# Three seven-product groups in each feed-forward step, and weight sums made by adding DMAs

## The chip, the cores and the metric

The kernel runs on one NeuronCore of a Trainium2 chip. The metric is the device time of one execution in microseconds. The kernel before takes 1654.93 us, the median of three runs (1654.54 to 1655.04).

## The reference

A two-layer encoder trunk on 256 tokens of 1024 channels, in float32. Each layer is a half-weighted feed-forward step, a mixer (an RG-LRU, a retention and a short convolution, gated and summed) and a second half-weighted feed-forward step; there are four feed-forward steps in all.

```python
def swiglu(u, w_in, w_out):
    gate, up = jnp.split(u @ w_in, 2, axis=-1)
    return (jax.nn.silu(gate) * up) @ w_out

for l in range(DEPTH):
    h = swiglu(rmsnorm(x, ffn1_pre_g[l]), ffn1_w_in[l], ffn1_w_out[l])
    x = x + 0.5 * rmsnorm(h, ffn1_post_g[l])
    h = hybrid_mixer(rmsnorm(x, mix_pre_g[l]), positions, ...)
    x = x + rmsnorm(h, mix_post_g[l])
    h = swiglu(rmsnorm(x, ffn2_pre_g[l]), ffn2_w_in[l], ffn2_w_out[l])
    x = x + 0.5 * rmsnorm(h, ffn2_post_g[l])
```

`w_in` is 1024 x 5632 (gate and up, 2816 each), `w_out` 2816 x 1024.

## The kernel before

**Precision.** Every float32 operand of a product is split into two parts: `hi`, the value cast to the matmul's format, and `lo`, the rest. A product is three matmuls (`mm3`, L457): hi x hi, hi x lo, lo x hi. Activations are split when they are transposed (`split`, L442), weights when they have been loaded.

**The weight stream.** All weights pass as 128x1024 units in one fixed order through the class `Stream`. `prep` (L153) loads a unit (two units per 1 MB DMA on SP's queue, tile `raw`), casts it on ACT to `whi` (L171) and subtracts on DVE to `wlo` (L172). There are eight buffers of each; `done` gives units back when the work that reads them has been written, and `fill` preps the next ones, at most eight ahead of the oldest that is still held.

**A feed-forward step** (`ffn`, L481) has eleven slices of 256 hidden channels. For a slice and one of the two token blocks of 128, `fin` is the input product (24 matmuls of 128x512 into one PSUM bank `psin`), `gate_up` the Silu on ACT and the product with up on DVE, `ftr` the transpose and split to `hl`, and `fout` the output product (12 matmuls into `psacc`, which collects over all slices). A slice's input costs 48 matmuls, its output 24. An input slice is four units, an output slice two.

**Seven products for eight.** For two slices c and d = c + 1, `block` computes the input product of the two token blocks, seen as a 2x2 times 2x2 block product, with seven products of 12 matmuls (P1 to P7, `product`, L519) in place of eight (2 x 48 = 96 matmuls). It needs four sums of the activations (`make_sums`, L350: two tiles `s`, each split again) and four sums of the weights. The weight blocks b[0] to b[3] are loaded as halves of 128x1024 into tiles `gw` (and one `w4`), and `part` (L178) forms the sums on DVE (L190 to L194) when P6 and P4 are prepped: four sums for each of two halves in each group. There are two groups in a step, (2, 3, 4, 5) and (6, 7, 8, 9) in `BLOCKS`, each with two slices a and b in the plain form between the products; slices 0, 1 and 10 are plain too. The results of the products are put together by `second`, `sixth`, `fifth` and `fourth` on DVE.

**What sets the order.** `ffn_plan` gives the order of the units, the code of `ffn` and `block` the order of the work; a scheduler then places the instructions in one queue per engine, and each engine runs its queue in that order. `turn` (an argument of `ffn`) transposes and splits the second token block of the step's input, and `first_sums` does the activation sums in the first step. POOL has only the powers of the RMS norms (L311, L389) and, in the first step, the constants of the LRU (`channel_consts`, L708); it issues no DMA.

## Time and profile before

| What | Value |
|---|---|
| Median of three runs | 1654.93 us |
| The profiled execution | 1654.75 us, its span 1653.0 us |
| PE busy | 1642.4 us (99% of the span), 7559 instructions |
| DVE busy | 1244.4 us (75%) |
| ACT busy | 920.7 us (56%) |
| POOL busy | 49.0 us (3%) |
| Moved by DMA | 309.85 MB, mean 187 GB/s |

PE is TensorE's matmul row, DVE the vector engine, ACT the scalar engine, POOL GpSimd, SP the engine that issues the weight loads. Busy matmuls overlap, so a busy share of 99% says that PE hardly waits, not that it is at its peak. The transposes of `turn` and their like (L370) stand in the chain of waits at 202.84, 657.22, 838.23, 1020.49 and 1475.10 us: the feed-forward steps take about 0 to 205 us, 650 to 838, 838 to 1020 and 1470 to 1653 of the span, and a mixer follows the first step of each layer.

### The profile page before, as it was taken

What the parts mean: (1) busy time and instruction counts of PE and PEld (TensorE: products, weight loads), DVE (VectorE), ACT (ScalarE), POOL (GpSimd) and SP (SyncE); (2) the same over time, 40 slices, a digit from 0 to 9 for tenths busy, and PEclk for the clock granted to TensorE, in tenths of its full rate; (3) what the DMA queues carried; (4) which work ended last, traced back from release to release, by engine and by line L of the source; (5) the groups of instructions that cost most, each with busy time, mean ns of one, the idle gap of its engine ahead of it and who ended that gap; (6) DMA issues with size and microseconds to landing.
All of it is one profiled execution on the core that took longest, in us unless ns stands there. A gap on an engine that the chain in (4) does not pass through costs nothing.

```text
span 1653.0 us, 19707 instructions
## 1 busy us (share of the span) xinstructions
PE 1642.4 (99%) x7559; PEld 1353.5 (82%) x7559; DVE 1244.4 (75%) x1596; ACT 920.7 (56%) x1249; POOL 49.0 (3%) x71
## 2 busy tenths in 40 slices
PE   9999999999999999999999999999999999999998
PEld 7888888888888888888888888888888888888886
DVE  7978779976666657878789777798566556688785
ACT  6556577654545445555556555766445545465553
POOL 0130000000000000000000000000000000000000
PEclk9999999999999999999999999999999999999999
DMA  9643554555454465464465444545554454645631
GB/s 332 245 180 147 207 177 174 208 183 204 159 197 153 179 241 204 169 239 176 170 240 191 153 153 179 203 153 208 200 196 161 170 186 155 256 169 185 215 109 69
DMA packets 50206, 309.85 MB, mean 187 GB/s; under 512 B 5696, under 2 KB 6080, under 8 KB 18112
## 3 DMA queue, kind: packets, MB, share of 16 engines
q1 hardware_dynamic: 47808, 301.18, 49.9%
q10 hardware_dynamic: 2304, 7.41, 1.2%
q8 instruction: 59, 0.97, 0.2%
q14 instruction: 35, 0.29, 0.1%
HBM read 307.52 MB, written 1.05 MB: 187 GB/s over the span
## 4 chain that ended last, share of the span: by engine, by line
PE 97%; DVE 2%; ACT 1%; issue 0%; DVEq 0%; POOLq 0%; ACTq 0%
PE psin L460 21%; PE psin L459 21%; PE psin L458 21%; PE psacc L458 9%; PE psacc L460 9%; PE psacc L459 9%; PE pstr L506 1%; PE pstr L773 1%; PE pstr L370 1%; DVE wlo L172 1%; PE pstr L941 0%; PE pstr L1020 0%; ACT whi L171 0%; PE psacc L290 0%; PE pstr L460 0%; PE pstr L458 0%
## 5 line engine op out<-in xcount | busy, mean ns | idle before, releaser
L172 DVE TENSOR_TENSOR wlo<-raw,whi 128x1024 fp32r<-128x1024 f32 x500 | 599.0, 1220 | 246.0 <-ACT whi L171 237.4
L171 ACT CAST whi<-raw 128x1024 fp32r<-128x1024 f32 x500 | 517.1, 1052 | 265.2 <-PE psacc L460 140.5
L458 PE MATMUL psin<-whi,uh 128*128 128x512 f32 x1424 | 561.0, 394 | 0.0
L459 PE MATMUL psin<-wlo,uh 128*128 128x512 f32 x1424 | 557.4, 391 | 0.5 <-DVE small L310 0.5
L460 PE MATMUL psin<-whi,ul 128*128 128x512 f32 x1424 | 556.9, 391 | 0.0
L460 PEld LDWEIGHTS psin<-whi,ul 128*128 128x128 f32 x1424 | 267.5, 188 | 55.6 <-DVE ul L445 0.5
L459 PEld LDWEIGHTS psin<-wlo,uh 128*128 128x128 f32 x1424 | 267.8, 188 | 54.1 <-DVE wlo L172 1.3
L458 PEld LDWEIGHTS psin<-whi,uh 128*128 128x128 f32 x1424 | 267.6, 188 | 53.2
L458 PE MATMUL psacc<-whi,hl 128*128 128x512 f32 x352 | 141.0, 401 | 0.9 <-ACT hl L444 0.5
L172 DVE TENSOR_TENSOR wlo<-gw,whi 128x1024 fp32r<-128x1024 f32 x96 | 116.1, 1220 | 30.3 <-ACT whi L171 30.3
L460 PE MATMUL psacc<-whi,hl 128*128 128x512 f32 x352 | 138.2, 393 | 0.0
L459 PE MATMUL psacc<-wlo,hl 128*128 128x512 f32 x352 | 137.5, 391 | 0.0
L171 ACT CAST whi<-gw 128x1024 fp32r<-128x1024 f32 x96 | 101.0, 1052 | 45.3 <-PE psin L460 24.7
L460 PE MATMUL psacc<-whi,spl 128*128 128x512 f32 x256 | 100.1, 391 | 0.0
L458 PE MATMUL psacc<-whi,spl 128*128 128x512 f32 x256 | 100.0, 390 | 0.0
L459 PE MATMUL psacc<-wlo,spl 128*128 128x512 f32 x256 | 99.8, 390 | 0.0
L458 PEld LDWEIGHTS psacc<-whi,hl 128*128 128x128 f32 x352 | 66.2, 188 | 15.3 <-ACT hl L444 3.4
L460 PEld LDWEIGHTS psacc<-whi,hl 128*128 128x128 f32 x352 | 66.1, 188 | 15.1 <-DVE hl L445 1.3
L459 PEld LDWEIGHTS psacc<-wlo,hl 128*128 128x128 f32 x352 | 66.3, 188 | 12.6
L311 POOL TENSOR_TENSOR small<-small,mhalf 128x1 f32<-128x1 f32 x38 | 29.5, 776 | 1521.9 <-DVE small L310 1521.0
L444 ACT CAST hl<-pstr 128x256 fp32r<-128x256 f32 x88 | 31.7, 370 | 55.2 <-PE pstr L506 55.2
L761 ACT COPY tok<-psin 128x512 f32<-128x512 f32 x40 | 23.4, 586 | 62.8 <-PE psin L460 62.8
(207 smaller groups left out, 1726.2 us busy)
## 6 DMA issues: line engine op xcount, KB each, us to landing
raw<-in_w_dram SPq DMA_DIRECT2D x250, 1024.0 KB, 4.8
gw<-in_w_dram SPq DMA_DIRECT2D x48, 512.0 KB, 6.9
w<-in_w_dram SPq DMA_DIRECT2D x16, 512.0 KB, 6.8
gain<-in_gains_dram ACTq DMA_DIRECT2D x10, 512.0 KB, 5.2
raw<-in_w_dram SPq DMA_DIRECT2D x8, 256.0 KB, 6.6
w<-in_gw_dram ACTq DMA_DIRECT2D x4, 512.0 KB, 3.4
x<-in_x_dram SPq DMA_DIRECT2D x2, 512.0 KB, 4.2
out_dram<-x SPq DMA_DIRECT2D x4, 256.0 KB, 2.1
```

Of the source, the lines that this page charges most:

```text
L171: (act or nc.scalar).copy(hi[:, c], raw[:, c])
L172: self.lows[i] = (dve or nc.vector).tensor_sub(lo[:, c], raw[:, c], hi[:, c].bitcast(F32))
L311: pool_e.tensor_tensor(r, r, mhalf, op=ALU.pow)
L370: pe.transpose(pt[:, i * P:(i + 1) * P], t[:, c * P:(c + 1) * P], ident)
L444: act.copy(h, src)
L458: pe.matmul(ps, lhsT=xh, rhs=wh, start=first, stop=False)
L459: pe.matmul(ps, lhsT=xh, rhs=wl, start=False, stop=False)
L460: pe.matmul(ps, lhsT=xl, rhs=wh, start=False, stop=last)
L506: pe.transpose(pt[:, i * P:(i + 1) * P], t[:, 256 + i * P:256 + (i + 1) * P], ident)
L761: act.copy(t, ps)
L773: pe.transpose(pt[:, i * SEQ + tb * P:i * SEQ + (tb + 1) * P], toks[tb][:, c * P:(c + 1) * P], ident)
```

## The change

There are three groups in each step, for the slice pairs (2, 3), (5, 6) and (8, 9), each with one plain slice a before it (1, 4, 7). The group with a = 1 comes first in the step and takes slice 0 into its order: P1 and P2 stand between the two token blocks of slice 0, and P3, P7 and P6 follow around slice 1. Another set of seven products is used. Per half it holds two tiles, x (from the block b11) and y (from b22), and z for b21, which is loaded whole into a `raw` tile. Weights of P1 are x, of P3 y, of P2 z. After P3's split a DMA that POOL issues adds b12 from memory into y; that is P7's operand. P6's is y + x, the one sum still made on DVE. After P6's split two more DMAs add b21 into y (for P4) and b12 into x (for P5). That is six adding DMAs of 512 KB in a group, 72 in all. The activation sums change their signs, and P1 to P7 are put together by other operations (`third`, `sixth`, `fifth`, `fourth`). In `channel_consts` the constants move from POOL to DVE, all but one power. `turn` is called within P2.

```diff
-PRODUCTS = (("P1", 2), ("P3", 0), ("P2", 3), ("P6", 2), ("P7", 0), ("P5", 1), ("P4", 3))
-SLOT = dict(PRODUCTS)
-BLOCKS = ((2, 3, 4, 5), (6, 7, 8, 9))
+PRODUCTS = ("P1", "P2", "P3", "P4", "P5", "P6", "P7")
+BLOCKS = ((1, 2, 3), (4, 5, 6), (7, 8, 9))
 def ffn_plan(blocks):
-    r, s = [], 0
-    while s <= NS:
-        block = [b for b in blocks if b[0] == s]
-        if block:
-            a, b, c, d = block[0]
-            r += [("in", a), ("P1", c), ("out", a - 1), ("P3", c), ("P2", c), ("in", b), ("P6", c), ("out", a),
-                  ("P7", c), ("out", b), ("P5", c), ("P4", c), ("out", c)]
-            s += 4
-            continue
-        if s < NS:
-            r.append(("in", s))
-        if s >= 1:
-            r.append(("out", s - 1))
-        s += 1
-    return r
+    r = [("in", 0)]
+    for a, c, d in blocks:
+        if a == 1:
+            r += [("P1", c), ("P2", c), ("in", a), ("P3", c), ("P7", c), ("P6", c), ("out", 0), ("out", a)]
+        else:
+            r += [("P3", c), ("P1", c), ("in", a), ("P7", c), ("P6", c), ("out", a - 1), ("P2", c), ("out", a)]
+        r += [("P4", c), ("P5", c), ("out", c)]
+    return r + [("in", NS - 1), ("out", NS - 2), ("out", NS - 1)]
...
             return piece
         piece(0)
-    def part(self, name, slot, half):
-        dve = self.nc.vector
-        if (name, half) == ("P1", 0):
-            self.group = [[None] * 4, [None] * 4]
-        b = self.group[half]
-        if name in ("P1", "P3"):
-            for k, q in enumerate((2, 0) if name == "P1" else (3, 1)):
-                b[q] = self.spare(name == "P3" and k == 1)
-                self.nc.sync.dma_start(b[q], self.w[self.pair, :, k * UW:(k + 1) * UW])
-            self.pair += 1
+        if kind is not None:
+            self.later(*kind)
+    def part(self, name, half):
+        if name in ("P1", "P3") and half == 0 and not self.open:
+            self.open = True
+            self.b11, self.b22, self.b21, self.b12 = [self.w[self.pair + k] for k in range(4)]
+            self.pair += 4
+            self.x, self.y = [None] * 2, [None] * 2
+        k = slice(half * UW, (half + 1) * UW)
+        if name == "P1":
+            self.x[half] = self.spare()
+            self.nc.sync.dma_start(self.x[half], self.b11[:, k])
+        elif name == "P3":
+            self.y[half] = self.spare()
+            self.nc.sync.dma_start(self.y[half], self.b22[:, k])
+        elif name == "P2":
+            if half == 0:
+                self.z = self.pool.tile([P, 2 * UW], F32, tag="raw", name=f"raw21_{self.pair}", bufs=RBUFS)
+                self.nc.sync.dma_start(self.z, self.b21)
+            return self.z[:, k]
         elif name == "P6":
-            dve.tensor_sub(b[0], b[0], b[1])
-            dve.tensor_sub(b[1], b[1], b[2])
-            dve.tensor_add(b[2], b[0], b[2])
-        elif name == "P4":
-            dve.tensor_sub(b[3], b[3], b[2])
-        return b[slot]
+            self.nc.vector.tensor_add(self.y[half], self.y[half], self.x[half])
+        return (self.x if name in ("P1", "P5") else self.y)[half]
+    def later(self, name, half):
+        def add(t, b):
+            self.nc.gpsimd.dma_start(t[half], b[:, half * UW:(half + 1) * UW], accum_op=ALU.add)
+        if name == "P3":
+            add(self.y, self.b12)
+        elif name == "P6":
+            add(self.y, self.b21)
+            add(self.x, self.b12)
+            self.open = False
...
         dve.tensor_sub(t[:, 0:2].rearrange("p c q t -> p q c t"), f, a)
-        dve.tensor_sub(t[:, 2], a[:, :, 1], t[:, 0])
-        dve.tensor_add(t[:, 1], t[:, 1], t[:, 0])
-        dve.tensor_add(t[:, 3], t[:, 2], f[:, :, 0])
+        dve.tensor_add(t[:, 2], t[:, 0], a[:, :, 1])
+        dve.tensor_sub(t[:, 1], t[:, 0], t[:, 1])
+        dve.tensor_sub(t[:, 3], t[:, 2], f[:, :, 0])
         h, lo = [tp.tile([P, 4, 2, P], F32R, tag="w4", name=nm("s"), bufs=8) for _ in range(2)]
         split(h, lo, t)
...
-        def block(a, b, c, d):
-            (u, v), (z, w) = halves(w4()), halves(w4())
+        def block(a, c, d):
+            (u, v), (z, w) = halves(w4()), [None] * 2
             def second(ps):
-                dve.tensor_add(z, u, ps)
-                gate_up(c, 0, [z])
+                t = v if a == 1 else u
+                dve.tensor_add(t, u, ps)
+                gate_up(c, 0, [t])
+            def third(ps):
+                nonlocal z, w
+                z, w = halves(w4())
+                act.copy(z, ps)
+            def fourth(ps):
+                dve.tensor_sub(z, ps, w)
+                gate_up(c, 1, [z])
+            def fifth(ps):
+                dve.tensor_sub(v, v, ps)
+                dve.tensor_sub(w, w, ps)
+                gate_up(d, 0, [v])
+                gate_up(d, 1, [w])
             def sixth(ps):
-                dve.tensor_add(u, u, ps)
-                dve.tensor_add(v, v, u)
-            def fifth(ps):
-                dve.tensor_add(v, v, ps)
-                dve.tensor_add(u, w, ps)
-                gate_up(d, 0, [v])
-                gate_up(d, 1, [u])
-            def fourth(ps):
-                dve.tensor_add(w, w, ps)
-                gate_up(c, 1, [w])
-            fin(a, 0)
-            fin(a, 1)
-            st.done(ui[a])
-            product(c, "P1", lambda ps: act.copy(u, ps))
-            fout(a - 1, 0)
-            ftr(a, 0)
-            fout(a - 1, 1)
-            ftr(a, 1)
-            st.done(uo[a - 1])
-            product(c, "P3", lambda ps: act.copy(v, ps))
-            product(c, "P2", second)
-            fin(b, 0)
-            fin(b, 1)
-            st.done(ui[b])
-            product(c, "P6", sixth)
-            fout(a, 0)
-            ftr(b, 0)
-            fout(a, 1)
-            ftr(b, 1)
-            st.done(uo[a])
-            product(c, "P7", lambda ps: dve.tensor_add(w, u, ps))
-            ftr(c, 0)
-            fout(b, 0)
-            fout(b, 1)
-            st.done(uo[b])
+                dve.tensor_sub(v, ps, u)
+                dve.tensor_sub(w, v, w)
+                dve.tensor_sub(v, v, z)
+            if a == 1:
+                product(c, "P1", lambda ps: act.copy(u, ps))
+                product(c, "P2", second, turn)
+                ftr(0, 0)
+                if start:
+                    first_sums()
+                else:
+                    fin(0, 1)
+                    st.done(ui[0])
+                fin(a, 0)
+                ftr(0, 1)
+                product(c, "P3", third)
+                ftr(a, 0)
+                fin(a, 1)
+                st.done(ui[a])
+                product(c, "P7", lambda ps: act.copy(w, ps))
+                product(c, "P6", sixth)
+                fout(0, 0)
+                ftr(c, 0)
+                fout(0, 1)
+                ftr(a, 1)
+                st.done(uo[0])
+                fout(a, 0)
+                fout(a, 1)
+                st.done(uo[a])
+            else:
+                product(c, "P3", third)
+                product(c, "P1", lambda ps: act.copy(u, ps))
+                fin(a, 0)
+                fin(a, 1)
+                st.done(ui[a])
+                product(c, "P7", lambda ps: act.copy(w, ps))
+                product(c, "P6", sixth)
+                fout(a - 1, 0)
+                ftr(a, 0)
+                fout(a - 1, 1)
+                ftr(a, 1)
+                st.done(uo[a - 1])
+                product(c, "P2", second)
+                fout(a, 0)
+                ftr(c, 0)
+                fout(a, 1)
+                st.done(uo[a])
+            product(c, "P4", fourth)
             product(c, "P5", fifth)
-            product(c, "P4", fourth)
             fout(c, 0)
+            ftr(c, 1)
             ftr(d, 0)
             ftr(d, 1)
-            ftr(c, 1)
             fout(c, 1)
             st.done(uo[c])
```

The order of the instructions, as the program has it. Names are tiles with their buffer numbers, DMASW is a semaphore of a DMA that POOL issued, DMAHW one of SP's or ACT's.

DVE in the first step, around the activation sums (`w_29`, `w_39`; `wlo` is a weight split). Before:

```order
L438 TENSOR_TENSOR w_28_313<-uh_115,ul_116 128x1024 [waits DVE_49]
L498 TENSOR_TENSOR tok_358<-psin_333,tok_358 128x256 [waits Activation_49]
L354 TENSOR_TENSOR w_29_315<-w_27_311,w_28_313 128x2x2x128 [waits DVE_49]
L445 TENSOR_TENSOR hl_364<-pstr_361,hl_364 128x256 [waits Activation_49]
L355 TENSOR_TENSOR w_29_315<-w_28_313,w_29_315 128x256 [waits DVE_49]
L356 TENSOR_TENSOR w_29_315<-w_29_315 128x256
L357 TENSOR_TENSOR w_29_315<-w_29_315,w_27_311 128x256 [waits DVE_49]
```

With the change (`gw_328` and `gw_335` are the halves of y):

```order
L447 TENSOR_TENSOR w_38_375<-uh_115,ul_116 128x1024
L454 TENSOR_TENSOR hl_370<-pstr_367,hl_370 128x256 [waits PE_49]
L165 TENSOR_TENSOR wlo_360<-gw_328,whi_359 128x1024 [waits DMASW0_49,Activation_49]
L363 TENSOR_TENSOR w_39_377<-w_37_373,w_38_375 128x2x2x128 [waits DVE_49]
L165 TENSOR_TENSOR wlo_364<-gw_335,whi_363 128x1024 [waits DMASW1_49,Activation_49]
L364 TENSOR_TENSOR w_39_377<-w_39_377,w_38_375 128x256 [waits DVE_49]
L365 TENSOR_TENSOR w_39_377<-w_39_377 128x256
L366 TENSOR_TENSOR w_39_377<-w_39_377,w_37_373 128x256 [waits DVE_49]
```

Both splits of P7, which wait for adding DMAs, now stand ahead of the three last operations of the activation sum.

DVE in the third feed-forward step (layer 1, the first step), where the results of products are put together and `hl`, the transposed hidden slices, are split. Before, in the first group:

```order
L545 TENSOR_TENSOR w_666_7213<-w_666_7213 128x512 [waits DVE_49]
L445 TENSOR_TENSOR hl_7532<-pstr_7529,hl_7532 128x256 [waits Activation_49]
L172 TENSOR_TENSOR wlo_7555<-gw_7271,whi_7554 128x1024 [waits Activation_49]
L445 TENSOR_TENSOR hl_7550<-pstr_7547,hl_7550 128x256 [waits Activation_49]
L172 TENSOR_TENSOR wlo_7560<-gw_7279,whi_7559 128x1024 [waits Activation_49]
L577 TENSOR_TENSOR w_667_7214<-w_666_7213,psin_7563 128x512 [waits PE_49]
```

With the change (`gw_7166`, `gw_7173` are y, for P4; `gw_6936`, `gw_6942` are x, for P5; `hl_7384` is slice 1 of the second token block):

```order
L165 TENSOR_TENSOR wlo_7320<-gw_7166,whi_7319 128x1024 [waits DMASW7_49,PE_49,Activation_49]
L165 TENSOR_TENSOR wlo_7324<-gw_7173,whi_7323 128x1024 [waits DMASW1_49,PE_49,Activation_49]
L571 TENSOR_TENSOR w_642_7046<-psin_7327,w_642_7046 128x512 [waits PE_49]
L165 TENSOR_TENSOR wlo_7344<-gw_6936,whi_7343 128x1024 [waits DMASW6_49,Activation_49]
L572 TENSOR_TENSOR w_667_7235<-w_642_7046,w_667_7235 128x512 [waits DVE_49]
L165 TENSOR_TENSOR wlo_7348<-gw_6942,whi_7347 128x1024 [waits DMASW0_49,Activation_49]
L573 TENSOR_TENSOR w_642_7046<-w_642_7046,w_667_7235 128x512 [waits DVE_49]
L454 TENSOR_TENSOR hl_7366<-pstr_7363,hl_7366 128x256 [waits Activation_49]
L454 TENSOR_TENSOR hl_7384<-pstr_7381,hl_7384 128x256 [waits Activation_49]
```

The weight splits near the `hl` rows waited for ACT alone; four that wait for adding DMAs now stand ahead of both.

POOL at the same place, before:

```order
L311 TENSOR_TENSOR small_6798<-small_6798,mhalf 128x1 [waits DVE_49]
L311 TENSOR_TENSOR small_6812<-small_6812,mhalf 128x1 [waits DVE_49,Pool_49]
L311 TENSOR_TENSOR small_6938<-small_6938,mhalf 128x1 [waits DVE_49]
L311 TENSOR_TENSOR small_6952<-small_6952,mhalf 128x1 [waits DVE_49,Pool_49]
L311 TENSOR_TENSOR small_8331<-small_8331,mhalf 128x1 [waits DVE_49,Pool_49]
```

With the change:

```order
L320 TENSOR_TENSOR small_6993<-small_6993,mhalf 128x1 [waits DVE_49]
L320 TENSOR_TENSOR small_7007<-small_7007,mhalf 128x1 [waits DVE_49,Pool_49]
L199 DMA gw_7166<-in_w_dram 128x1024 [waits DMASW4_49,DMAHW3_49,DVE_49,Activation_49]
L199 DMA gw_7173<-in_w_dram 128x1024 [waits DMASW5_49,DMASW2_49,DMAHW2_49,DVE_49,Activation_49]
L199 DMA gw_6936<-in_w_dram 128x1024 [waits DMAHW1_49,DMASW6_49,DVE_49]
L199 DMA gw_7166<-in_w_dram 128x1024 [waits DMASW7_49,DVE_49]
L199 DMA gw_6942<-in_w_dram 128x1024 [waits DMASW0_49,DVE_49]
L199 DMA gw_7173<-in_w_dram 128x1024 [waits DMASW1_49,DVE_49]
```

Between the powers of the norms POOL's queue now has the adds of the group, each behind a wait for DVE.

## Rows read from the trace of the kernel before

**Rows 1.** The page: span, engines' busy time, the weight queue, the chain by engine.

```profile
span 1653.0 us, 19707 instructions
...
PE 1642.4 (99%) x7559; PEld 1353.5 (82%) x7559; DVE 1244.4 (75%) x1596; ACT 920.7 (56%) x1249; POOL 49.0 (3%) x71
...
q1 hardware_dynamic: 47808, 301.18, 49.9%
...
PE 97%; DVE 2%; ACT 1%; issue 0%; DVEq 0%; POOLq 0%; ACTq 0%
```

**Rows 2.** Who waited for whom, PE alone: us in total, times, longest us.

```profile
PE psacc L290 <- DVE ones L287: 1.4, 1, 1.4
PE psin L127 <- DVE ul L127: 0.5, 1, 0.5
PE psacc L458 <- ACT hl L444: 0.5, 1, 0.5
PE psin L127 <- ACT uh L127: 0.5, 1, 0.5
PE psin L459 <- DVE small L310: 0.5, 2, 0.2
PE psin L127 <- DVE wlo L127: 0.2, 1, 0.2
```

**Rows 3.** Timeline of PE in the first step: start us, us, instruction.

```profile
23.49 0.49 PE L458 MATMUL psin<-whi,uh 128*128 128x512 f32 x1
23.82 0.39 PE L459 MATMUL psin<-wlo,uh 128*128 128x512 f32 x1
...
28.84 0.39 PE L460 MATMUL psin<-whi,ul 128*128 128x512 f32 x1
```

**Rows 4.** Timelines of ACT, then DVE, in the first step.

```profile
20.34 2.00 ACT L171 CAST whi<-raw 128x1024 fp32r<-128x1024 f32 x2
...
23.69 0.41 ACT L497 ACTIVATE tok<-psin 128x256 f32<-128x256 f32 x1
...
24.81 3.48 DVE L172 TENSOR_TENSOR wlo<-raw,whi 128x1024 fp32r<-128x1024 f32 x3
...
33.09 0.68 DVE L354 TENSOR_TENSOR w<-w,w 128x512 f32<-128x512 f32 x1
33.69 0.42 DVE L445 TENSOR_TENSOR hl<-pstr,hl 128x256 fp32r<-128x256 f32 x1
34.02 0.42 DVE L355 TENSOR_TENSOR w<-w,w 128x256 f32<-128x256 f32 x1
```

**Rows 5.** Weight loads: one tile's, then issues in windows 700:760 and 20:50, the page.

```profile
DMA to landing us min/median/max: 3.4/6.9/10.1
...
gw<-in_w_dram SPq DMA_DIRECT2D x6, 512.0 KB, 6.1
...
gw<-in_w_dram SPq DMA_DIRECT2D x4, 512.0 KB, 8.3
...
raw<-in_w_dram SPq DMA_DIRECT2D x250, 1024.0 KB, 4.8
```

**Rows 6.** Windows of the first step: busy by engine, granted clock, DMA share, GB/s.

```profile
25.00:30.00 5.00, 5.00 (x25) 4.10 (x24) 5.00 (x5) 3.95 (x6) 0.00 (x0) 1.00 0.96 354
30.00:35.00 5.00, 5.00 (x24) 4.06 (x23) 5.00 (x9) 3.52 (x5) 0.00 (x0) 1.00 0.99 359
```

**Rows 7.** Windows at the end, then the timeline of PE's opening.

```profile
1646.00:1647.00 1.00, 0.68 (x3) 0.20 (x2) 0.66 (x1) 0.59 (x3) 0.00 (x0) 1.00 0.00 0
...
1648.00:1649.00 1.00, 0.00 (x0) 0.00 (x0) 0.87 (x2) 0.00 (x0) 0.34 (x1) 0.88 0.00 0
1649.00:1650.00 1.00, 0.00 (x0) 0.00 (x0) 0.79 (x2) 0.00 (x0) 0.00 (x0) 0.50 0.03 10
...
1.44 6.25 PE L290 MATMUL psacc<-ones 128*128 128x512 f32 x15 [1.44 <-DVE ones L287]
7.53 1.04 PE L127 MATMUL pstr<-ident,w 128*128 128x128 f32 x8
```

93 lines of the change are left out of this document (35 added, 58 removed).

## The prediction

> **What bounds the kernel now.** Start with the page's first table [rows 1]: TensorE (PE) is busy 1642.4 us of a span of 1653.0, and the chain that ended last is 97% PE. DVE is at 75%, ACT at 56%, POOL at 3%. The view of who waited for whom, for PE alone [rows 2], lists six waits, the longest 1.4 us, at the start. So PE's instruction stream is the time: a matmul less is time less, and a wait of PE is time more. DVE and ACT work ahead of it; each weight unit is split there (cast to `whi`, subtract to `wlo`) up to eight units before PE reads it.
>
> The mean of one 128x512 matmul in the list of lines (391 ns) is no price, since matmuls overlap. In the timeline of PE the starts go from 23.82 to 28.84 with 22 steps between them [rows 3]: 5.02 / 22 = 0.228 us each. That is the price used here. In the same way the timelines of ACT and DVE give what one more instruction costs in a queue [rows 4]: a cast of a unit 0.95 us (two in 2.00), a 128x1024 subtract or add 1.14 (three in 3.48), a 128x512 operation 0.60, a 128x256 one 0.33. A transpose on PE costs 0.13 (eight in 1.04 [rows 7]).
>
> **What the change removes.** A seven-product group needs 84 matmuls where two slices need 96. There are two groups per feed-forward step before, three after, four steps: 4 x 12 = 48 matmuls less, 48 x 0.228 = 10.9 us. It is all on the path.
>
> **What costs nothing by itself.** DVE loses 40 weight sums (64 to 24) at 1.14 us, 45.6 us, and gets 24 unit splits more, 27.4 us; ACT gets 24 casts, 22.8 us. Neither engine is full, and the prefetch of eight units hides it; where it doesn't, it is in the deadlines below. The LRU constants come back to DVE as some 25 short operations in the first step; 1.0 us of them stands in a deadline below. `turn` keeps its place in time: 39 matmuls after the step's first one (24 + 15 before, 24 + 12 + 3 after). Loaded data grows by some 24 MB to about 334 MB, over queues that are used 50% [rows 1].
>
> **What it adds: 72 adding DMAs on POOL's queue, and waits for them.** No row of the trace shows such a DMA. Call L the time from the moment its last reader on DVE is done to its landing. The nearest rows are the plain 512 KB loads of the same tiles [rows 5]: 3.4 us at the fastest, 10.1 at the slowest; median 6.1 in a stretch inside a feed-forward step, 8.3 at the start, where the DMA engines are 0.96 to 0.99 busy [rows 6]. I take the medians of the place, 6.1 and 8.3, and keep 3.4 and 10.1 as the ends.
>
> In groups two and three P3 and P7 start 72 matmuls apart (16.4 us), and from P6's end to P4 there are 60 (13.7 us); no cost up to L = 10. The first group of each step is different: P3, P7 and P6 follow each other closely, and each is the last sum plus one more matrix.
>
> *Steps two to four* (time from the first matmul of slice 0). Slice 0 of the second token block ends after 72 matmuls and some ten transposes, 17.8. DVE then has, in its order, the gate product (with ACT's Silu 0.6), two splits of slice 1, a split of the input sums, and the split of P3's first half: 18.4 + 4 x 1.14 = 23.0. Only then can the first add into `y` start; it lands at 23.0 + L. Behind it stand, one after the other, cast 0.95, split, P6's own sum, split, split, gate product, sum, cast, split: 6 x 1.14 + 2 x 0.95 + 0.33 = 9.1. So P6's last weights are ready at 32.1 + L. PE wants them after 96 + 48 matmuls, fourteen transposes and 7 matmuls of P6, at 36.3. **PE waits L - 4.2.** Then the second adds: the last one into `y` starts at 32.1 + L and lands at 32.1 + 2L. The second order block of the section on the change shows what is queued behind it on DVE: its split, P6's three PSUM operations with the two splits of P5 between them, and the two `hl` splits, the second of which the output product of slice 1 needs. With the cast that is 0.95 + 3 x 1.14 + 3 x 0.60 + 2 x 0.33 = 6.8, so 38.9 + 2L; PE has 53 matmuls and four transposes from 32.1 + L on, to 44.7 + L. **PE waits L - 5.8.** With L = 6.1: 1.9 + 0.3 = 2.2 per step, 6.6 in three.
>
> *The first step* has the worse order [the first order block]: on DVE the splits of P7, which wait for the adds, stand ahead of the sums of the activations, without which P3 can't begin. Before, the activation sums wait for nothing but DVE. From the rows at 23.69 on ACT and 24.81 on DVE [rows 4], 7 splits follow (24.8 + 7 x 1.14 = 32.8); the second add starts there and lands at 33.0 + L = T. After it the queue runs through a cast, six operations of 1.14, nine of 0.33 and one of 0.60, and the last split of the activation sums is done at T + 11.4 (the last split of P6 one later, T + 12.5, which frees the second add); P3 and the half of slice 1 that is mixed into it on PE end 9 matmuls later, T + 13.5. Without the wait they end after 48 + 36 matmuls from 23.5 [rows 3] and four transposes, 43.2. **PE waits L + 3.3**, 11.6 with L = 8.3. At the second adds a cast, four splits, three PSUM operations, two `hl` splits and 1.0 of constants (9.0) follow the landing at T + 12.5 + L, and PE needs the result 62 matmuls and four transposes after T + 13.5, at T + 28.2: L - 6.7, 1.6. A wait this long also lowers the clock: at the end of the trace the granted clock goes from 1.00 to 0.50 some 2 us after PE's last matmul [rows 7], and the 15 opening matmuls take 6.25 us, 0.417 each. If as many run at that rate after the wait, 15 x (0.417 - 0.228) = 2.8. Sum of the first step: 16.0.
>
> **The sum.** The profiled execution took 1654.75 us (1653.0 span and 1.75 around it), 0.18 below the median of the three runs. 1654.75 - 10.9 + 6.6 + 16.0 = 1666.5; I say **1666**. Ends: with L = 3.4 the first step costs 6.7 and the others nothing, 1650.5, and with every wait hidden 1643.8. With L = 10.1 the steps cost 3 x (5.9 + 4.3) and 13.4 + 3.4 + 2.8, 1694; with the clock's 2.8 in each step too, 1702.
>
> **Two rules of the Trainium skill.** In "DMA: Bandwidth & Descriptors", Anatomy of one DMA — SWDGE (gpsimd) path, a DMA from GpSimd is put at about 2.0 us plus bytes over 436e3 per us; for 512 KB my estimate from it is 3.2 us. The sum by it is the lower end's, about 1650; the fastest plain load here, 3.4, agrees, the medians do not, and no run here shows a DMA from POOL. Against the change speaks "Collectives: The Full Stack", The bandwidth ceiling: the fold count and why AG ≠ RS ≠ AR: a DMA that adds reads two sources, and is half as fast as a copy. No row here shows it.
>
> **Rivals.**
> - *The adds land fast.* For it: 3.4 us is there when a load is alone [rows 5], and POOL's queue has nothing else. Against: in these stretches loads run. 1644 to 1651, faster.
> - *The add costs like a load of twice the bytes, and no more.* The 1 MB loads take 4.8 [rows 5]. Then the steps cost 3 x 0.6, the first 8.1 + 2.8, and gain and waits cancel: 1656.5, no change.
> - *The adds are slow*, 10 us or more. For it: the DMA engines are nearly full at the start [rows 6], and four adds stand behind each other within some 6 us. Against: later in the steps the loads take 6.1. From L = 7 on the later steps alone cost the whole gain (3 x (2.8 + 1.2) = 12.0): 1694 to 1702 at L = 10.1.
> - *The prefetch hides the first groups anyway*, because ACT and DVE run ahead more than I count. For it: PE hardly waits in the kernel before [rows 2]. Against: the 23.0 comes from a queue in which the gate product waits for PE itself. It ends with the first rival.
>
> **How the numbers follow.** Forecast (L from 5.5 to 9) 0.56; slow adds 0.20; cancelling 0.12; fast or hidden 0.12. About 0.2%, 3.3 us, is what a measurement of this kernel tells from no change. Slower than that: the first two, 0.76; within it 0.12; faster 0.12. The range from 1648 to 1702 leaves out half of the fast case and the far end of the slow one. The likeliest case alone reaches from 1660 to 1686.
>
> **What would show it.** PE's waits, now 3.6 us in all, should be some 20 us, in the first group of each step: half of it before P3 in the first step (near 36 us from the start), named as waits for ACT's and DVE's splits of `s`; the rest at P6 and at the second half of the output product of slice 1, named `wlo` and `hl`. ACT and DVE should show waits for the adding DMAs there, and none that reach PE in groups two and three. PE's instructions go down by 48. The median landing of the adds decides: under 4.5 us I am wrong towards faster, over 9 towards slower. I am also wrong if PE waits little although the adds take 6 us or more: then my count of the queues is too long.

## The result and the profile after

The kernel after takes **1711.88 us** (median of four runs, 1710.05 to 1715.66) against 1654.84 before: a ratio of 1.0348 [1.033, 1.0366], slower. The direction was forecast, the size was not: 1666 was predicted, and the range ended at 1702.

The profiled execution took 1712.71, 57.96 more than before's 1654.75. The page of the kernel after: span, busy time, the granted clock in 40 slices, the DMA queues, the chain by engine, and the loads with their median landing. They answer to [rows 1] and [rows 5].

```profile
span 1710.9 us, 19924 instructions
...
PE 1649.9 (96%) x7511; PEld 1351.8 (79%) x7511; DVE 1250.6 (73%) x1631; ACT 955.8 (56%) x1293; POOL 96.6 (6%) x119
...
PEclk9799999999999999999999999999999999999999
...
q1 hardware_dynamic: 44928, 288.60, 45.8%
q0 software_dynamic: 10368, 37.75, 12.3%
...
PE 83%; DVE 5%; DMA 5%; issue 3%; ACT 2%; POOL 1%; POOLq 0%; DVEq 0%; ACTq 0%; SPq 0%
...
raw<-in_w_dram SPq DMA_DIRECT2D x246, 1024.0 KB, 4.9
gw<-in_w_dram POOLq DMA_DIRECT2D x72, 512.0 KB, 7.2
gw<-in_w_dram SPq DMA_DIRECT2D x48, 512.0 KB, 6.4
```

PE has 48 matmuls less, and yet its busy time is 7.5 us longer: part of the rest ran at a lower clock (below). The chain, 97% PE before, now passes through DVE and DMA. The new queue q0 holds the 72 adding DMAs. Its 37.75 MB take 12.3% of the 16 DMA engines' span, 210 us, so **2.92 us of all 16 engines for each add of 512 KB**. On SP's queue the same bytes cost 1.42 (45.8% of 1710.9, for 550 times 512 KB).

Who waited for whom, PE of the kernel after (us in total, times, longest us), to be held against [rows 2]:

```profile
PE psacc L467 <- ACT hl L453: 17.4, 4, 6.4
PE pstr L515 <- DVE tok L507: 15.4, 2, 14.8
PE psacc L469 <- DVE hl L454: 6.6, 1, 6.6
PE psin L468 <- DVE wlo L165: 3.5, 5, 0.8
PE psin L467 <- ACT whi L164: 2.3, 4, 0.6
PE psin L467 <- ACT w L576: 1.9, 2, 1.1
PE pstr L379 <- DVE w L342: 1.5, 2, 1.1
```

The waits come to 54.0 us in all against 3.6 before. The first three lines hold 39.4 of them: one wait of 14.8 us in the first step, and one before slice 1's second output product in each step (`hl`: 6.6, 5.8, 6.4, 4.7). They stand where the prediction put its waits, though the `hl` waits of the later steps were put at 0.3 each.

The first wait, in the timelines of PE, POOL, ACT and DVE (start us, us, instruction; in brackets the idle time before it and who ended it):

```profile
34.98 0.38 PE L515 MATMUL pstr<-ident,tok 128*128 128x128 f32 x2
50.13 0.90 PE L515 MATMUL pstr<-ident,tok 128*128 128x128 f32 x3 [14.78 <-DVE tok L507]
...
51.47 0.63 PE L468 MATMUL psin<-wlo,s 128*128 128x512 f32 x1
51.89 0.63 PE L467 MATMUL psin<-whi,uh 128*128 128x512 f32 x1
52.32 0.63 PE L468 MATMUL psin<-wlo,uh 128*128 128x512 f32 x1
```
```profile
32.24 2.00 POOL L199 DMA_DIRECT2D gw<-in_w_dram  x2 [23.93 <-DVE wlo L165]
```
```profile
42.54 1.04 ACT L164 CAST whi<-gw 128x1024 fp32r<-128x1024 f32 x1 [6.72 <-DMA gw<-in_w_dram]
...
46.44 1.04 ACT L164 CAST whi<-gw 128x1024 fp32r<-128x1024 f32 x1 [2.85 <-DMA gw<-in_w_dram]
```
```profile
43.62 1.23 DVE L165 TENSOR_TENSOR wlo<-gw,whi 128x1024 fp32r<-128x1024 f32 x1 [7.04 <-ACT whi L164]
47.51 1.23 DVE L165 TENSOR_TENSOR wlo<-gw,whi 128x1024 fp32r<-128x1024 f32 x1 [2.06 <-ACT whi L164]
49.66 0.41 DVE L507 TENSOR_TENSOR tok<-psin,tok 128x256 f32<-128x256 f32 x1
```

POOL issues the first two adds when DVE has read their tiles. The second is issued at 33.36 and lands 13 us later, beside the start's loads; ACT casts it, DVE splits it at 47.51, and only then comes the operation on `tok` that PE has waited for since 35.4: the chain of the first order block. Afterwards PE's matmuls start 0.42 to 0.43 us apart instead of 0.228. The windows (busy by engine, granted clock, DMA share, GB/s) show why:

```profile
37.00:40.00 3.00, 0.00 (x0) 0.00 (x0) 0.00 (x0) 0.00 (x0) 0.00 (x0) 1.00 1.02 258
40.00:43.00 3.00, 0.00 (x0) 0.00 (x0) 0.00 (x0) 0.46 (x1) 0.00 (x0) 0.55 1.07 281
...
52.00:55.00 3.00, 3.00 (x11) 2.38 (x10) 3.00 (x7) 0.30 (x1) 0.71 (x1) 0.68 0.48 70
```

PE idles, the granted clock falls to 0.50, the lower of its two levels (1.2 GHz), and is not back at once when the work is. The DMA engines meanwhile are full: what is late is the transfer.

**A later step**, the one that starts near 650 us: POOL's timeline around 700, the landing of the last add of its first group (window 712:713), and the waiting matmul of PE.

```profile
697.03 0.90 POOL L199 DMA_DIRECT2D gw<-in_w_dram  x1 [15.97 <-DVE wlo L165]
699.30 0.86 POOL L199 DMA_DIRECT2D gw<-in_w_dram  x1 [1.37 <-DVE tok L507]
706.48 0.86 POOL L199 DMA_DIRECT2D gw<-in_w_dram  x1 [6.32 <-DVE gw L193]
708.90 0.86 POOL L199 DMA_DIRECT2D gw<-in_w_dram  x1 [1.55 <-DVE wlo L165]
710.04 0.86 POOL L199 DMA_DIRECT2D gw<-in_w_dram  x1 [0.28 <-DVE gw L193]
712.38 0.86 POOL L199 DMA_DIRECT2D gw<-in_w_dram  x1 [1.47 <-DVE wlo L165]
```
```profile
DMA to landing us min/median/max: 11.4/11.4/11.4
```
```profile
728.30 0.80 PE L467 MATMUL psacc<-whi,hl 128*128 128x512 f32 x1 [5.84 <-ACT hl L453]
```

The six adds land after 5.4, 5.8, 5.3, 5.5, 8.3 and 11.4 us: alone, or some 2.3 us behind one other, an add takes 5.3 to 5.8; the third and fourth of four that are issued within 6 us take 8.3 and 11.4.

**Where the 57.96 us went.** PE's waits +50.4 (54.0 less 3.6). Behind the opening, 83 of the 128x512 matmuls are followed by a start more than 0.36 us later (waits left out), with 17.2 us beyond 0.228, against 11 with 2.1 before. Of the 83, 53 with 11.5 us lie in the six stretches in which the granted clock is 0.50; the other 30, with 5.8 us, lie at the full clock, as all 11 of before do. So the lower clock costs +11.5, and wide starts at the full clock +3.7. The 48 matmuls: -10.9. The remaining +3.3 is in transposes and smaller gaps that no row names.

### The profile page after: what moved, and what is told of

Read it like the earlier page. It is cut to its first block, busy times and chain, and to the rows that moved or that the text cites. A ratio compares the mean times of both kernels' runs of the same rounds, so it can differ in the third digit from the quotient of the medians.

```text
span 1710.9 us, 19924 instructions
## 1 busy us (share of the span) xinstructions
PE 1649.9 (96%) x7511; PEld 1351.8 (79%) x7511; DVE 1250.6 (73%) x1631; ACT 955.8 (56%) x1293; POOL 96.6 (6%) x119
## 3 DMA queue, kind: packets, MB, share of 16 engines
q1 hardware_dynamic: 44928, 288.60, 45.8%
q0 software_dynamic: 10368, 37.75, 12.3%
## 4 chain that ended last, share of the span: by engine, by line
PE 83%; DVE 5%; DMA 5%; issue 3%; ACT 2%; POOL 1%; POOLq 0%; DVEq 0%; ACTq 0%; SPq 0%
PE psin L467 18%; PE psin L469 18%; PE psin L468 18%; PE psacc L467 8%; PE psacc L469 8%; PE psacc L468 8%; DMA gw<-in_w_dram 5%; DVE wlo L165 2%; ACT whi L164 1%; PE pstr L515 1%; PE pstr L781 1%; PE pstr L379 1%; POOL gw L199 0%; PE pstr L1028 0%; PE pstr L949 0%
## 5 line engine op out<-in xcount | busy, mean ns | idle before, releaser
L467 PE MATMUL psin<-whi,uh 128*128 128x512 f32 x1344 | 531.8, 396 | 1.9 <-ACT w L576 1.9
L468 PE MATMUL psin<-wlo,uh 128*128 128x512 f32 x1344 | 526.6, 392 | 0.5 <-DVE wlo L165 0.5
L469 PE MATMUL psin<-whi,ul 128*128 128x512 f32 x1344 | 526.1, 391 | 0.0
L469 PEld LDWEIGHTS psin<-whi,ul 128*128 128x128 f32 x1344 | 253.5, 189 | 52.9
L468 PEld LDWEIGHTS psin<-wlo,uh 128*128 128x128 f32 x1344 | 254.0, 189 | 51.2 <-DVE wlo L165 0.9
L165 DVE TENSOR_TENSOR wlo<-gw,whi 128x1024 fp32r<-128x1024 f32 x144 | 173.4, 1221 | 79.4 <-ACT whi L164 78.7
L164 ACT CAST whi<-gw 128x1024 fp32r<-128x1024 f32 x144 | 148.9, 1051 | 128.9 <-DMA gw<-in_w_dram 62.2
L467 PE MATMUL psacc<-whi,hl 128*128 128x512 f32 x352 | 143.5, 409 | 17.8 <-ACT hl L453 17.4
L199 POOL DMA_DIRECT2D gw<-in_w_dram x72 | 62.6, 875 | 439.4 <-DVE wlo L165 268.7
L467 PE MATMUL psin<-whi,s 128*128 128x512 f32 x192 | 77.3, 403 | 3.5 <-ACT whi L164 2.3
L468 PE MATMUL psin<-wlo,s 128*128 128x512 f32 x192 | 75.8, 395 | 3.1 <-DVE wlo L165 3.0
```

Source lines behind the costliest of these rows:

```text
L164: (act or nc.scalar).copy(hi[:, c], raw[:, c])
L165: self.lows[i] = (dve or nc.vector).tensor_sub(lo[:, c], raw[:, c], hi[:, c].bitcast(F32))
L199: self.nc.gpsimd.dma_start(t[half], b[:, half * UW:(half + 1) * UW], accum_op=ALU.add)
L467: pe.matmul(ps, lhsT=xh, rhs=wh, start=first, stop=False)
L468: pe.matmul(ps, lhsT=xh, rhs=wl, start=False, stop=False)
L469: pe.matmul(ps, lhsT=xl, rhs=wh, start=False, stop=last)
```

## The experiments

The theory ahead of the first runs (A): the cost is in the adding DMAs, their time on the engines and what queues behind them on DVE. The rival (R): the new order of the first group costs it, whatever makes the sums. Kernels run with the kernel before on the same chip (1654.5 to 1654.8). Their diffs are against the kernel after, shortened to the lines that carry the edit; medians in us, the ratio to before in brackets. "Idle" is the sum of PE's waits in the profiled execution.

### Are the adds the cost?

**e1_no_adds.** No weight sums but P6's on DVE.

```diff
-            add(self.y, self.b12)      # after P3
-            add(self.y, self.b21)      # after P6
-            add(self.x, self.b12)
```


> The changed kernel with the 72 adding DMAs left out (P7, P4 and P5 then use sums that lack b12 or b21; all else as it is). Theory A, the landing of the adds is the whole loss: what remains is the gain of 48 matmuls, 10.9 us, less a wait of some 4 us in the first step, where the splits of P7 still stand ahead of the activation sums: 1645 to 1650 us, PE's waits under 10 us, the granted clock hardly below 1. Theory R, the new structure costs by itself (order of the products, copies on ACT, the constants on DVE): 1680 us or more, with PE waits at the same places.

1664.49 [1.0046, 1.0076], idle 18.5. Between the two. The adds cost 1711.88 - 1664.49 = 47.4; but without them 20.7 us remain above the 1643.8 that the matmuls alone would give (1654.75 - 10.9), so R holds for a part.

**e2_plain_loads.** The same DMAs, without adding.

```diff
-  self.nc.gpsimd.dma_start(t[half], b[...], accum_op=ALU.add)
+  self.nc.gpsimd.dma_start(t[half], b[...])
```


> The changed kernel with the 72 DMAs on POOL's queue as plain loads that overwrite their tile in place of adding to it; order and waits are the same. Theory A1, an adding DMA lands late because it takes the DMA engines twice as long as a load (in the profile of the changed kernel 2.9 us of all 16 engines for each 512 KB against 1.4): the median from issue to landing falls from 7.2 to about 5 us, the first wait of PE from 14.8 to about 9, and the time to 1675 to 1690 us. Theory A2, any DMA at that place and from that queue lands as late, behind the loads that SP issues: the median stays near 7 us and the time at 1700 to 1715 us.

1676.51 [1.0117, 1.0147]. The page's lines of its queue and landing:

```profile
q0 software_dynamic: 10368, 37.75, 6.9%
...
gw<-in_w_dram POOLq DMA_DIRECT2D x72, 512.0 KB, 5.3
```

Against 12.3% and 7.2 above: the same bytes and issues cost 1.60 us of all engines (6.9% of 1674.5 over 72) where they don't add, 2.92 where they do. Of the 47.4 us the transfers are 12.0 and the adding 35.4. The median landing, 5.3, is as theory A1 had it; the first wait fell to 11.2, not to the 9 that it expected.

**e3_sums_on_dve.** b12 and b21 loaded into spare tiles, the 72 sums on DVE.

```diff
-  self.nc.gpsimd.dma_start(t[half], b[...], accum_op=ALU.add)
+  self.nc.vector.tensor_add(t[half], t[half], b)
```


> The changed kernel with the 72 adding DMAs replaced by loads of b12 and b21 on SP's queue, made with those of y, and 72 more sums on DVE (each 1.14 us in its queue); three groups in each step as in the change. Theory A: DVE is not full and the sums are ready in time but for the first step: 1645 to 1656 us, faster than or level with the kernel before. Theory R (structure): 1680 us or more. Theory F, DVE is the new limit (72 x 1.14 = 82 us more on an engine that is busy 73%): PE waits for DVE's splits in all three groups, 1665 to 1700 us.

1679.44 [1.013, 1.0164], idle 28.8, DVE busy 1322.3. 32 us better than with adding DMAs, 15 worse than without sums, in the range of theory F. The loads of b12 and b21 that come with the sums are not tested apart.

### Which adds?

**e7_no_first_adds.** No adding DMA in the first group of each step; the 48 of groups two and three stay.

```diff
-        if name == "P3":
+        if name == "P3" and not first:
             add(self.y, self.b12)
...
+            if not first:      # after P6
```


> The changed kernel with the 24 adds of the first group of each step left out (its P7, P4 and P5 use sums that lack b12 or b21); the 48 of groups two and three remain. Theory G, only the first groups are short of time: 1662 to 1668 us, as without any adds (1664.5). Rival: the adds of the later groups cost as well, by their waits or by the DMA time that they take from loads: 1675 us or more.

1666.65 [1.0058, 1.0092]: 2.2 above e1. So in this layout 24 adds cost 45.2 us and 48 cost 2, as the prediction had it for groups two and three.

**e5_no_x_adds.** Only the adds into `y`.

```diff
             add(self.y, self.b21)
-            add(self.x, self.b12)
```


> The changed kernel with only the 24 adds of b12 into x left out (P5 then uses x as loaded; 48 adds remain). In the changed kernel four adds stand behind each other in the first group of the third step, issued within 6 us, and land after 5.3, 5.5, 8.3 and 11.4 us; PE waits 5.8 us for what is queued behind the last. Theory S, the four share the DMA engines (2.9 us of all 16 for each): with two of them gone the last add into y lands after 5.5 to 6.5 us, the waits of 4.7 to 6.4 us at hl in steps two to four go, with the half clock behind them: 1682 to 1692 us. Theory Q, the loads from SP's queue hold it up: the last add still takes 10 us or more, 1703 to 1712 us.

1685.27 [1.017, 1.02], 26.6 better. Near 700 us the second adds into `y`, issued at 701.88 and 705.36, now land after 5.5 and 5.6 us, as the first pair does. The view of landings for the later one, and the share of the 16 engines of each queue from 701 to 711 (q0 has the adds, q1 SP's loads):

```profile
DMA to landing us min/median/max: 5.6/5.6/5.6
...
q0 software_dynamic: 288, 1.05, 59.1%
q1 hardware_dynamic: 32, 0.26, 8.9%
```

Against 5.5 and 11.4 us with the adds into `x` between them. The two have the engines nearly to themselves, and the `hl` waits of the later steps, 4.7 to 6.4 us in the kernel after, are down to 0.5. The adds into `x`, which P5 needs, had delayed the one into `y` that P4 needs sooner.

### What is in the order of the first step?

**e4_consts_late.** The LRU constants move to the third group.

```diff
-            if b[0] == 4 and during is not None:
+            if b[0] == 7 and during is not None:
```


> The changed kernel with the LRU constants' operations on DVE placed in the third group of the first step in place of the first; their loads stay where they are. In the changed kernel the second half of hl of slice 1 stands behind a wait of 2.9 us for POOL's power and 1.1 us of constants, and PE waits 6.6 us there. Theory C, this order is a cost of its own beside the adds: the wait falls to 2 to 3 us and the stretch at half clock behind it shrinks: 1700 to 1708 us. Theory A alone (the landing sets that wait): no change, 1710 to 1715 us.

1707.97 [1.0309, 1.035], 3.9 better, but the runs overlap (1706.24 to 1714.30, against 1710.05 to 1715.66 of the kernel after). What the trace shows is clearer: the first step's `hl` wait fell from 6.6 to 3.0, and a new wait of 2.0 stands in the third group, as it does in e6, e8, e11 and e12 with the constants at the same place. What had stood in DVE's queue is in the kernel after's timelines of POOL and DVE:

```profile
77.03 2.93 POOL L725 TENSOR_TENSOR cc<-base,cc 128x16 f32<-128x16 f32 x1 [16.58 <-DVE cc L723]
```
```profile
76.08 0.42 DVE L454 TENSOR_TENSOR hl<-pstr,hl 128x256 fp32r<-128x256 f32 x1
80.00 0.17 DVE L727 TENSOR_SCALAR cc<-cc 128x16 f32<-128x16 f32 x1 [2.94 <-POOL cc L725]
81.45 0.41 DVE L454 TENSOR_TENSOR hl<-pstr,hl 128x256 fp32r<-128x256 f32 x1
```

DVE waits 2.94 us for POOL's one power, between the two `hl` halves.

**e6_sums_first.** Besides, DVE's activation sums go ahead of the weight splits that wait for the adds.

```diff
-                    first_sums()
+                    ready = first_sums()
+                with tc.issue_after(ready[0].ins), tc.issue_after(ready[1].ins):
+                    st.done(up[("P2", c)])
```


> The changed kernel with the constants late as in e4, and in the first step the casts and splits of P7's weights placed behind the activation sums and their splits; all adds stay. Theory H, what costs there is the order (sums that wait for nothing stand behind splits that wait for the adds): the wait of 14.8 us before P3 shrinks to 4 to 6 us, some of it comes back at P7 and at the next adds, which start earlier against PE: 1696 to 1703 us, against 1708 for e4. Theory D, P7 needs the two adds as soon as P3 is done, so that order moves the wait and no more: 1705 to 1710 us, the wait at P7 in place of P3.

1704.8 [1.0276, 1.032], between the two theories. The wait before P3 is 2.2 + 0.9 instead of 14.8, and yet only 3.2 us are won over e4: an 8.25 us wait stands at `hl` in its place (3.0 in e4). The adds are late still, and the next reader pays.

**e9_p3_early.** P3's weights ahead of slice 1's, so that the first adds start sooner.

```diff
-  r += [("P1", c), ("P2", c), ("in", a), ("P3", c), ...]
+  r += [("P1", c), ("P2", c), ("P3", c), ("in", a), ...]
```


> The changed kernel with P3's two units placed four units earlier in the weight stream of the first group (ahead of slice 1's input units in place of behind them); products, adds and all else as they are. Theory E, the adds are late because they start only when P3's weights are split, and that waits for its turn in the eight buffers: the first pair of adds starts some 4 to 5 us earlier, the wait of 14.8 us in the first step falls to about 10 and those of 4.7 to 6.4 us at hl in steps two to four to under 2: 1680 to 1692 us. Rival: an earlier add only meets more loads and lands when it did before: 1702 to 1712 us.

1707.46 [1.0293, 1.0333]; the theory falls. The first pair was issued 4.5 us sooner, at 27.75, and landed after 9.9 and 13.8 us, the second 3.7 us sooner than in the kernel after (42.7 against 46.4). Yet PE still waited 13.2: in this order ACT's first operation for `tok` stands behind the second cast of P7's weights (43.69 behind 42.74), and more of the activation sums stand behind the splits on DVE. So the wait there is not the landing alone. In the later steps the last of the four adds took 13.4 to 13.8 us, and the `hl` waits stayed at some 6 us a step (3.3 and 3.0 in the step near 700).

**e11_no_adds_ordered.** e1 with the edits of e6.

> No adding DMAs, as in e1 (1664.5 us; P7, P4 and P5 use sums that lack b12 or b21), with the activation sums ahead of P7's splits and the constants late as in e6. If the loss that is left there beside the adds is the order of DVE's queue in the first step (waits of 3.9, 1.4, 1.4 and 1.2 us and two stretches at half clock): 1656 to 1661 us. If it is the closeness of P3, P7 and P6 itself, DVE being full there: 1663 to 1667 us.

1660.48 [1.0021, 1.0047], 4.0 below e1, as expected. It is still slower than before, with no weight sums but P6's: PE's waits are 17.4 us.

### Other ways to make the sums

**e8_hybrid.** e6, with DVE's sums in the first group of each step and adding DMAs in the others.

```diff
+        if self.groups % 3 == 0:
+            self.nc.vector.tensor_add(t[half], t[half], c[half])   # P7, P4, P5
```


> Three groups in each step; the first group's sums on DVE from loads of b12 and b21, made when P7, P4 and P5 are prepared; adding DMAs in groups two and three; the constants late and the activation sums ahead of P7's splits as in e6. By the theories H and G together: of the 18.5 us that PE waits without any adds some 8 go, and the 24 more sums of the first groups cost a little: 1652 to 1660 us, level with the kernel before. If DVE's queue in the first groups is the limit (the runs with all sums on DVE took 1679): 1668 to 1680 us.

1682.47 [1.0155, 1.0185]; a miss. The waits went into groups two and three (2.78 at 117.8, 3.7 around 1585).

**e10_all_mended.** e6 and e9 together, P5's sum on DVE.

```diff
+        elif name == "P5":
+            self.nc.vector.tensor_add(self.x[half], self.x[half], self.c12[half])
```


> P3's units early as in e9, the activation sums ahead of P7's splits and the constants late as in e6, and the sum for P5 on DVE from a load of b12 (48 adding DMAs remain, all into y). If the causes found so far (the four adds that share the DMA engines, the order in the first step, the late start) are all there is beside what the kernel without adds loses: 1658 to 1668 us. If the adds of y alone still set the first groups: 1675 us or more. Under 1650 us would mean that the 48 matmuls' gain comes through.

1690.12 [1.0196, 1.0227]; a miss. By what was expected at 1675 and above, the adds into `y` alone still set the first groups (`hl` waits of 3.5 to 3.8 us in the three later steps).

### A layout with room between the products

The next kernels give the first group another order, in which the products that need sums stand further apart; `turn` moves from P2 into slice 1, e11's queue order is kept, and from e13 on the LRU constants come in two parts, at the second and the third group.

```diff
-  r += [("P1", c), ("P2", c), ("in", a), ("P3", c), ("P7", c), ("P6", c), ("out", 0), ("out", a)]
+  r += [("in", a), ("P3", c), ("P1", c), ("out", 0), ("P7", c), ("P6", c), ("P2", c), ("out", a)]
```

**e12_room** (all adds as DMAs)

> The first group of each step laid out anew, all 72 adds kept: slice 0 and slice 1 are opened plainly as in the kernel before (the second token block is turned within slice 1), then P3, P1, half of slice 0's output, P7, P6, the other half, P2, slice 1's output, P4, P5. From the end of slice 0's input, where P3's weights are split, to P7 PE has 60 matmuls in place of 36, and P3 follows 24 matmuls of slice 1; from P6 to P4 there are 48. Constants late and the activation sums ahead of P7's splits as in e6. Theory G+S, the adds cost only where PE has too little between their start and their use: with landings of 5.5 to 8 us the waits nearly go, and the 10.9 us of the matmuls come through: 1645 to 1652 us, faster than the kernel before. If landings of 10 us and more (first step, fourth of four adds) still reach PE: 1655 to 1670 us. If an adding DMA costs wherever it stands: 1685 us or more.

1689.71 [1.0205, 1.0233], 22 better than the kernel after but a miss. In the first step four adds are issued within 4 us and land after up to 15.1; `hl` waits 4.5, 6.1 and 4.4 in the steps.

**e13_room_two_adds** (the first groups' sums into `x` on DVE, so that two adds stand behind each other instead of four)

```diff
+        elif name == "P5" and self.groups % 3 == 0:
+            self.nc.vector.tensor_add(self.x[half], self.x[half], self.c12[half])
```


> As e12, but in the first group of each step the sum for P5 is made on DVE from a load of b12 (64 adds remain; in these groups two stand behind each other before P4 in place of four), and the constants' power is started in group two, so that the rest in group three does not wait for it. Theory S (the burst of four adds): the last add into y lands after 6 to 8 us in place of 15, the waits of 4.4 to 6.1 us at hl and those of 7 us around P4 in the first step go with their stretches at half clock: 1647 to 1655 us. If loads in flight hold up even two adds (10 us or more): 1660 to 1680 us.

1690.17 [1.0188, 1.0224]; a miss. The landings of the two adds that are issued at 700.56 and 701.70, and the queues' shares of the engines from 700 to 714:

```profile
DMA to landing us min/median/max: 8.9/10.8/12.7
...
q1 hardware_dynamic: 398, 2.41, 45.7%
q0 software_dynamic: 287, 1.05, 45.4%
```

Two adds are nearly as late, up to 12.7 us, as four (14.4 in the later steps of e12) where SP's loads run beside them. Here SP issues two 1 MB loads at 703.70, and they share the engines with the adds; in e5 it did so at 707.36, when the later add was nearly through. So other adds are not needed to make an add late: loads do it too. And the delay has moved: in the first step's second group four adds go out within 1.7 us, the last lands after 19.4, and PE waits 4.9 there.

**e14_room_no_adds**

> The layout of e12 without any adding DMA (P7, P4 and P5 use sums that lack b12 or b21), constants as in e13: the floor of this layout. Theory G (the waits that were left without adds came from P3, P7 and P6 standing close and from the turn within P2): 1645 to 1649 us, the 10.9 us of the 48 matmuls nearly whole. If the seven-product group in the first place costs by itself: 1655 us or more.

**1647.6 [0.9944, 0.9969], faster than before**, idle 6.3, without the sums. Its page:

```profile
PE 1631.6 (99%) x7511; PEld 1343.2 (82%) x7511; DVE 1248.3 (76%) x1631; ACT 955.2 (58%) x1293; POOL 34.9 (2%) x47
```

PE is at 99% as before, and 7 of the 10.9 us arrive. The gain of the matmuls is real; the layout of the kernel after, with the constants in its third group, took 13 us more (e11 less e14). The sums must come for under 7.

**e15_room_dve** (all 96 sums on DVE)

```diff
+        if name in ("P7", "P4", "P5"):
+            self.nc.vector.tensor_add(t[half], t[half], c)
```


> The layout of e14 with all sums on DVE: b12 is loaded beside y on SP's queue, b21 is read from the tile that P2 uses, so no byte is loaded twice and no adding DMA is left; 96 sums on DVE in place of 64 in the kernel before. Theory: DVE (75% busy before, some 78% then) has the room in this layout, and PE's waits stay under 12 us: 1648 to 1653 us, faster than the kernel before. Rival: DVE's queue in the groups is the limit, as in e3 (15 us above the same kernel without sums): 1657 to 1668 us.

1669.22 [1.0077, 1.0105], the best with all sums, still slower than before. DVE is busy 1323.5 us, 79%, and idle is 18.7. The first lines of PE's waits:

```profile
PE pstr L520 <- DVE tok L512: 5.3, 4, 1.8
PE psin L473 <- DVE wlo L165: 3.4, 5, 1.8
PE psin L472 <- DVE w L571: 2.9, 4, 0.8
```

No wait of 5 us, but many of about one, for `tok`, for splits and for the operations that put the products together (`w`): by these names they stand in DVE's queue behind the sums. The waits make 12.4 of the 21.6 us over e14. The loads of b12 are not tested apart, but with them the kernel moves 309.86 MB, as the kernel before does.

**e16_room_hybrid** (e15 in the first groups, adding DMAs in the others)

> As e15 in the first group of each step; adding DMAs in groups two and three (48 of them). Theory G, those groups have the time: within 3 us of e15. Rival: the adds there take DMA time from the loads and come late themselves once the groups before run undisturbed: 8 us or more above e15, with PE's waits in groups two and three.

1692.89 [1.0205, 1.0246]; a miss. The 48 adds that cost 2 us in e7 cost 23.7 over e15 here: one of 5.0 at 116 us, 2.8 at 766, 955 and 1598 among the waits. The first of these waits follows four adds that go out within 1.7 us; the last lands after 19.5. What hides an add is its surroundings, not its group's number.

**e17_room_pool** (e15, P5's 24 sums as POOL's own adds)

```diff
+  (self.nc.gpsimd if name == "P5" else self.nc.vector).tensor_tensor(t[half], t[half], c, op=ALU.add)
```


> As e15, with the 24 sums for P5 made by POOL's own adds in place of DVE's (no adding DMA). If DVE's queue is what costs in e15, a quarter of the sums less gives back a good part: 1655 to 1663 us. If POOL's add of 128x1024 is slow (no row has shown one) or slows DVE beside it: 1669 us or more, and PE waits at P5.

1710.49 [1.0329, 1.0357], 41 slower than e15. Its list of lines, POOL's sums and then DVE's splits of the same tiles; behind them the second for e15 (busy us, mean ns, idle before):

```profile
L200 POOL TENSOR_TENSOR gw<-gw,gw 128x1024 f32<-128x1024 f32 x24 | 75.2, 3141 | 411.6 <-DVE gw L196 326.9 <-ACT whi L164 41.5 <-DMA raw<-in_w_dram 22.5
...
L165 DVE TENSOR_TENSOR wlo<-gw,whi 128x1024 fp32r<-128x1024 f32 x144 | 215.0, 1517 | 13.3 <-ACT whi L164 12.5
```
```profile
L165 DVE TENSOR_TENSOR wlo<-gw,whi 128x1024 fp32r<-128x1024 f32 x144 | 172.1, 1217 | 2.0 <-ACT whi L164 1.6
```

A sum takes 3.14 us in the mean on POOL against 1.21 on DVE, and DVE's own splits of `gw` rise from 1217 to 1517 ns: 43 us more on DVE where 29 were to be taken off it. The mean hides two kinds. 21 of the 144 splits begin while a POOL sum has 2 us or more to go: they take 3.10 to 3.43 us and end 1.08 to 1.09 us after the sum, each time. The other 123 take 1.20 to 1.23. One pair, POOL's sum and DVE's split:

```profile
798.05 3.19 POOL L200 TENSOR_TENSOR gw<-gw,gw 128x1024 f32<-128x1024 f32 x1 [3.57 <-issue]
```
```profile
799.01 3.31 DVE L165 TENSOR_TENSOR wlo<-gw,whi 128x1024 fp32r<-128x1024 f32 x1
```

So in this trace DVE's split stands still until POOL's sum is over. The four `tok` operations that began beside a sum, which read PSUM and one tile, took their usual 0.42.

## Why the prediction was wrong in size

- **The 48 matmuls, 10.9 us**: right. The instruction count is 7511, and e14 comes within 4 us of the whole of it.
- **The queues behind the adds**: right in their places, in part by luck in their length. With the measured times put into the prediction's own formulas: first wait L + 3.3 with L = 13.2 gives 16.5 (measured 14.8); P6 in the step at 700 with L = 5.8 gives 1.6 (1.1); the `hl` waits of the three later steps, with L = 11.4, 11.9 and 10.2, give 5.6, 6.1 and 4.4 (5.84, 6.37, 4.70). The luck is in the last. In the step at 700 the wait ends with ACT's cast for `hl`, 4.4 us after the landing, not with DVE's split at the 6.8 that was counted; and PE comes to it after 41 matmuls, not the 53 of the sum. One error takes 2.4 us off the wait, the other puts 2.7 on. The names did not all come as told: PE waits for `tok` in the first step, not for splits of `s`, and for `tok` again at P6 in the step at 700.
- **One L for every add: the step that failed.** The medians of the plain loads, 6.1 and 8.3, were taken for all. An add costs the engines twice a load (2.92 us against 1.42 on SP's queue, 1.60 in e2) and lands after 5.3 us at best (3.9 in e2). And the adds that PE waits for are not median ones: the first pair lands in the start's loads after 10 to 13 us, the last of each first group behind other transfers after 10.1 to 11.9. The median, 7.2, was in the forecast's band; the late tail set the time. The largest part of the 46 us that were missing is there: the `hl` waits of the three later steps were priced at 3 x 0.3 = 0.9 and came as 16.9. The first wait, 11.6 in the sum, came as 14.8. The rival "the adds are slow" had these figures (10.1 and its 1694 to 1702) and was held back by "later in the steps the loads take 6.1", a median again. e5, where the last add into `y` lands after 5.6 and the `hl` waits of the later steps are gone, gives 26.6 us back; e13 shows that loads beside two adds make such a tail too.
- **The second wait of the first step**, L - 6.7: 10.1 - 6.7 = 3.4 was to come, 6.6 came. The constants were priced at 1.0; POOL's power holds DVE for 2.94 (e4: the wait falls to 3.0).
- **The clock**, 2.8 in the first step alone: 11.5 came. The price of a stretch was not too low (11.5 / 6 = 1.9), their number was: each of the five waits of 4.7 us and more was followed by one, and so were the shorter waits around `turn` near 681. Only the range's far end priced the clock in every step, at 11.2.
- **`turn` keeps its place**, and so was priced at nothing: around it stand waits of 4.1 us in three steps (in the list of waits the transposes behind `w` L342, 1.5, those behind `w` L576, 0.7, and the products behind `w` L576, 1.9). Of the 20.7 us of e1 the order of DVE's queue with the constants' place makes 4.0 (e11), the layout 12.9 (e11 to e14), and 3.8 are left in e14. The 12.9 hold the order of the products, the place of `turn` and the constants in two parts, which no run takes apart. Without adds this alone eats the gain, and the prediction missed it.
- **Groups two and three cost nothing**: right here (2.2, e7), not a property of the groups (e16).
- **The two rules of the Trainium skill.** The Trainium skill, "Collectives: The Full Stack", The bandwidth ceiling: the fold count and why AG ≠ RS ≠ AR, says of the reduce step of a ring that its add needs two source reads and that it runs at half the copy's rate. These traces agree for a kernel's own adding DMA: 2.92 us against 1.60 and 1.42 is 1.8 to 2.05 times. The estimate of 3.2 us that the prediction made from the Trainium skill, "DMA: Bandwidth & Descriptors", Anatomy of one DMA — SWDGE (gpsimd) path, is not met: a DMA from this queue landed after 5.3 us at the fastest where it adds, and where it doesn't after 3.9 at the fastest and 5.3 at the median (e2).

What stays open: the 3.7 us of wide starts at the full clock and the 3.3 of transposes and small gaps, and whether some order of the first groups brings the sums in for under the 7 us that e14 leaves. Of the kernels tried none with all sums beats the kernel before.

## What to carry to other kernels

Price a transfer on the path by the landing of the last one in its burst, beside the loads that run there, not by a median over a stretch; and take an adding DMA, for the engines' time, as a load of twice its bytes. Where matmuls are saved by an algebraic trick, ask which engine makes the sums and which short operations stand behind them in its queue: first run the kernel with the sums left out (here 7 us of gain), then ask whether any engine can make them for less. And waits of TensorE can cost more than their length: here 50 us of them brought 11.5 more by the lower clock.
